# Mean of relu over rows: 126 rows a partition, and two blocks of 128 rows in the first load

## The chip, the cores, the metric

One core of one Trainium2 chip. The metric is the device time of one execution in microseconds (us); the median of several executions is given. Lower is better. The profile's own span begins with the first instruction and ends with the last, and is about 1.3 us shorter than that execution's time (159.8 against 161.13 us for the profiled run of the kernel before).

The kernel spreads its rows over 128 partitions of the on-chip memory (the first number in shapes such as 128x1024). Of the engines, ACT is ScalarE, DVE is VectorE, POOL is GpSimd, and SP is the one that issues the transfers here. A *run* is one contiguous stretch of bytes that one DMA engine moves as one transfer. A *semaphore* is a counter by which a finished load, or a finished instruction, is told to whoever waits for it.

## The reference

```python
# x: (32, 512, 1024) float32, that is 16384 rows of 1024 numbers, 4 KB each
relu_x = np.maximum(x, 0)
return np.mean(relu_x, axis=-1).astype(np.float32)     # (32, 512)
```

67.11 MB are read once, 64 KB are written.

## The kernel before

The first 128 rows are an early block, one row to a partition. Of the other 16256 rows each partition has 127 consecutive ones. They come as seven tiles of 16 rows (a run of 64 KB for each partition, three buffers), then as pieces of 7, 4, 2 and 1 rows, and the last row in three pieces by columns. All loads are issued by the SP engine on one queue. ACT reduces the even rows, DVE the odd ones; the one-row piece (the *split row* below) is shared, 448 columns for ACT and 576 for DVE.

```python
xfirst, xmain = xf[:P, :], xf[P:, :]
outfirst, outmain = out.flatten()[:P], out.flatten()[P:]
J = J - 1                                               # 127
xr = xmain.rearrange("(p j) d -> p j d", p=P, j=J)      # pitch between partitions: 127 rows
...
NB, BUFS = 16, 3                                        # (two lines in the kernel)
full = J // NB                                          # 7
row_pieces = [7, 4, 2, 1]
col_pieces = [512, 256, 256]
...
for t in range(full):
    buf_free(t)                                         # waits for ACT and DVE, from t = 3
    if t == 0:
        load(-1, row0[:, :], xfirst)                    # early block
    load(t, bufs[t % BUFS][:, :, :], xr[:, t * NB:(t + 1) * NB, :])
    if t == BUFS:
        nc.sync.wait_ge(first, 2)
        nc.sync.dma_start(                              # the early block's 128 means
            out=outfirst.rearrange("(q i) -> q i", i=32), in_=turned0[0:P:32, :],
        ).then_inc(stored, 16)
...                                                     # loads of the pieces
nc.scalar.activation(                                   # early block, on ACT
    out=row0[:, :], in_=row0[:, :], func=ACT.Relu, scale=inv, accum_out=mean0[:, 0:1],
).then_inc(first, 1)
nc.vector.wait_ge(first, 1)
nc.vector.transpose(turned0[:, :], mean0[:, :]).then_inc(first, 1)
for t in range(full):
    rows(t, bufs[t % BUFS], 0, NB, t * NB)              # 8 rows on ACT, 8 on DVE
...
dve_row(nc, last[:, 512:768], last[:, D + 1:D + 2]).then_inc(dve, 1)     # "256-wide"
...
nc.vector.scalar_tensor_tensor(                         # the last one: 256 columns and two partial sums
    out=last[:, 768:], in0=last[:, 768:], scalar=0.0, in1=scale[:, :], op0=ALU.max, op1=ALU.mult,
    accum_out=res[:, J - 1:J],
).then_inc(dve, 1)
...
nc.sync.dma_start(out=outr[:, j0:], in_=res[:, j0:]).then_inc(stored, 16)   # last store
```

## Time and profile before

| | before |
|---|---|
| time, three runs | 161.34 us (161.02 to 161.39) |
| span of the profiled run | 159.8 us |
| share of the span: DMA queue, DVE, ACT | 97.9%, 46%, 44% |
| first load byte to last (single transfers) | 1.44 to 157.56 us |
| one 64 KB run, median | 2418 ns |

The shares of a span are averages. "Single transfers" are the records that the trace keeps for each run a DMA engine moved: start, duration, size. They do not name the engine. Their times are given here, and in the prediction, on a scale on which the last record ends with the span. As the trace keeps them they stand 0.40 to 0.45 us earlier on the scale of the timeline (1.01 to 157.13 us for the kernel before). Durations and streams do not depend on this, but the gap between a single transfer and an instruction does.

### The profile page before, as it was taken

Reading aid. Unit: us, or ns where it says so; the run is one execution under the profiler, and the core shown is the slowest. Engines: PE = TensorE matmul, PEld = TensorE weight load, DVE = VectorE, ACT = ScalarE, POOL = GpSimd, SP = SyncE. Lnnn points to the kernel's source line nnn. Section 1 sums busy time; section 2 is a strip of 40 time slices with the busy share of each in tenths; the row PEclk is TensorE's granted clock in tenths of the full one; section 3 lists DMA queues with packets and bytes.
Section 4 is the critical chain, followed back from the end, with each engine's and each line's share of the span. In section 5 each row is a group of like instructions: output and inputs, shape, how many; then the busy total and the mean of one; then the engine's idle time right before and its main releaser. Section 6 shows DMA issues by size and latency. Waiting matters only on the chain. (4 is left out here: it accounts for less than half of the span.)

```text
span 159.8 us, 348 instructions
## 1 busy us (share of the span) xinstructions
DVE 73.3 (46%) x131; ACT 70.4 (44%) x133; POOL 1.3 (1%) x9
## 2 busy tenths in 40 slices
DVE  0000029900399005970079500894009920199975
ACT  1400029800397005950079300892009900199974
POOL 1000000000000000000000000000000000000001
DMA  9979989999799699699699699799899997998993
GB/s 394 459 328 525 410 377 525 394 394 525 345 443 525 263 525 525 263 525 525 263 525 509 279 525 476 312 525 427 361 525 394 394 525 328 427 438 382 414 411 110
DMA packets 2456, 67.18 MB, mean 420 GB/s; under 512 B 536, under 2 KB 792, under 8 KB 1176
## 3 DMA queue, kind: packets, MB, share of 16 engines
q1 hardware_dynamic: 2456, 67.18, 97.9%
HBM read 67.11 MB, written 0.07 MB: 420 GB/s over the span
## 5 line engine op out<-in xcount | busy, mean ns | idle before, releaser
L20 DVE TENSOR_SCALAR_CACHE_REDUCE rows<-rows 128x1024 f32<-128x1024 f32 (+1 forms) x63 | 72.1, 1209 | 78.8 <-DMA rows<-in_x_dram 78.6
L15 ACT ACTIVATE rows<-rows 128x1024 f32<-128x1024 f32 x64 | 66.2, 1035 | 84.0 <-DMA rows<-in_x_dram 83.8
L15 ACT ACTIVATION_READ_ACCUMULATOR rows<-rows 128x1 f32 x64 | 11.9, 186 | 0.0
L20 DVE DVE_READ_ACCUMULATOR rows<-rows 128x1 f32 x63 | 5.2, 83 | 0.0
L168 DVE STREAM_TRANSPOSE turned<-mean 128x32 f32<-128x32 f32 x1 | 0.2, 211 | 5.9 <-ACT row L164 5.9
L164 ACT ACT_TABLE_LOAD x1 | 1.3, 1283 | 3.3 <-DMA row<-in_x_dram 3.3
L157 POOL TENSOR_SCALAR res<-sums 128x112 f32<-128x112 f32 (+1 forms) x2 | 0.5, 249 | 153.8 <-DVE rows L20 153.8
L164 ACT ACTIVATE row<-row 128x1024 f32<-128x1024 f32 x1 | 1.1, 1056 | 0.0
L15 ACT ACTIVATE last<-last 128x512 f32<-128x512 f32 x1 | 0.6, 629 | 0.0
L20 DVE TENSOR_SCALAR_CACHE_REDUCE last<-last 128x256 f32<-128x256 f32 x1 | 0.4, 420 | 0.3 <-DMA last<-in_x_dram 0.3
L197 DVE SCALAR_TENSOR_TENSOR last<-last,scale 128x258 f32<-128x258 f32 x1 | 0.4, 428 | 0.1
L142 POOL MEMSET scale<- 128x258 f32 x1 | 0.3, 313 | 0.0
L187 POOL TENSOR_SCALAR res<-part 128x1 f32<-128x1 f32 x1 | 0.3, 266 | 0.6 <-DVE rows L20 0.6
L164 ACT ACTIVATION_READ_ACCUMULATOR row<-row 128x1 f32 x1 | 0.2, 187 | 0.0
L15 ACT ACTIVATION_READ_ACCUMULATOR last<-last 128x1 f32 x1 | 0.2, 186 | 0.0
L141 POOL MEMSET mean<- 128x32 f32 x1 | 0.1, 125 | 1.5 <-POOLq L55 1.5
L235 POOL MEMSET const-bfloat16-1.0<- 128x1 bf16 x1 | 0.1, 103 | 0.0
L235 POOL MEMSET const-uint8-127<- 128x1 uint8 x1 | 0.1, 103 | 0.0
L235 POOL MEMSET const-float32-0.0<- 128x1 f32 x1 | 0.1, 99 | 0.2 <-issue 0.2
L235 POOL MEMSET const-float32-1.0<- 128x1 f32 x1 | 0.1, 99 | 0.0
L20 DVE DVE_READ_ACCUMULATOR last<-last 128x1 f32 x1 | 0.1, 83 | 0.0
L197 DVE DVE_READ_ACCUMULATOR last<-last,scale 128x1 f32 x1 | 0.1, 82 | 0.0
## 6 DMA issues: line engine op xcount, KB each, us to landing
rows<-in_x_dram SPq DMA_DIRECT2D x1, 3584.0 KB, 37.9
rows<-in_x_dram SPq DMA_DIRECT2D x1, 2048.0 KB, 42.4
rows<-in_x_dram SPq DMA_DIRECT2D x1, 1024.0 KB, 44.5
row<-in_x_dram SPq DMA_DIRECT2D x1, 512.0 KB, 3.2
rows<-in_x_dram SPq DMA_DIRECT2D x1, 512.0 KB, 45.3
last<-in_x_dram SPq DMA_DIRECT2D x1, 256.0 KB, 45.5
last<-in_x_dram SPq DMA_DIRECT2D x2, 128.0 KB, 45.2
rows<-in_x_dram SPq DMA_DIRECT2D x7, 48.7
```

Of the source, the lines that this page charges most:

```text
L15: return nc.scalar.activation(out=src, in_=src, func=ACT.Relu, accum_out=acc)
L20: return nc.vector.tensor_scalar(out=src, in0=src, scalar1=0.0, scalar2=init, op0=ALU.max, op1=ALU.add, accum_out=acc,)
L141: nc.gpsimd.memset(mean0[:, :], 0.0)
L142: nc.gpsimd.memset(scale[:, :], inv).then_inc(pool, 1)
L157: nc.gpsimd.tensor_scalar(out=res[:, lo:hi], in0=sums[:, lo:hi], scalar1=inv, scalar2=0.0, op0=ALU.mult, op1=ALU.add,).then_inc(pool, 1)
L164: nc.scalar.activation(out=row0[:, :], in_=row0[:, :], func=ACT.Relu, scale=inv, accum_out=mean0[:, 0:1],).then_inc(first, 1)
L168: nc.vector.transpose(turned0[:, :], mean0[:, :]).then_inc(first, 1)
L187: nc.gpsimd.tensor_scalar(out=res[:, J - 2:J - 1], in0=part[:, 0:1], scalar1=part[:, 1:2], scalar2=inv, op0=ALU.add, op1=ALU.mult,).then_i ...
L197: nc.vector.scalar_tensor_tensor(out=last[:, 768:], in0=last[:, 768:], scalar=0.0, in1=scale[:, :], op0=ALU.max, op1=ALU.mult, accum_out=r ...
L235: nc = _bacc.Bacc("TRN2", target_bir_lowering=False, num_devices=1)
```

## The change

Intent, as far as the source tells it: one more row of every partition goes into the early load, which makes the rest an even 126 rows and shortens the first piece behind the tiles and the last store.

```diff
-    xfirst, xmain = xf[:P, :], xf[P:, :]
-    outfirst, outmain = out.flatten()[:P], out.flatten()[P:]
-    J = J - 1
+    xfirst, xmain = xf[:2 * P, :].rearrange("(c p) d -> p c d", c=2), xf[2 * P:, :]
+    outfirst, outmain = out.flatten()[:2 * P], out.flatten()[2 * P:]
+    J = J - 2
...
-    row_pieces = [7, 4, 2, 1]
+    row_pieces = [6, 4, 2, 1]
...
-            nc.sync.dma_start(
-                out=outfirst.rearrange("(q i) -> q i", i=32), in_=turned0[0:P:32, :],
-            ).then_inc(stored, 16)
+            for c in range(2):
+                nc.sync.dma_start(
+                    out=outfirst[c * P:(c + 1) * P].rearrange("(q i) -> q i", i=32), in_=turned0[c:P:32, :],
+                ).then_inc(stored, 16)
...
-    nc.scalar.activation(
-        out=row0[:, :], in_=row0[:, :], func=ACT.Relu, scale=inv, accum_out=mean0[:, 0:1],
-    ).then_inc(first, 1)
+    for c in range(2):
+        done = nc.scalar.activation(
+            out=row0[:, c, :], in_=row0[:, c, :], func=ACT.Relu, scale=inv, accum_out=mean0[:, c:c + 1],
+        )
+    done.then_inc(first, 1)
```

(Cut: the shape of `row0`, the argument of the first load, the final count of `stored`.)

More of the change, by code (lines that the diff above doesn't have):

```diff
@@ L88 @@
     scale = sbuf("scale", P, D // 4 + 2)
-    row0, mean0, turned0 = sbuf("row0", P, D), sbuf("mean0", P, 32), sbuf("turned0", P, 32)
+    row0, mean0, turned0 = sbuf("row0", P, 2, D), sbuf("mean0", P, 32), sbuf("turned0", P, 32)
     loaded = [nc.alloc_semaphore(f"loaded{i}") for i in range(full + len(row_pieces) + len(col_pieces) + 1)]
@@ L119 @@
         if t == 0:
-            load(-1, row0[:, :], xfirst)
+            load(-1, row0[:, :, :], xfirst)
         load(t, bufs[t % BUFS][:, :, :], xr[:, t * NB:(t + 1) * NB, :])
@@ L212 @@
     nc.sync.sem_clear(range(used[0], used[-1] + 1))
-    nc.sync.wait_ge(stored, 48).then_inc(stored, -48)
+    nc.sync.wait_ge(stored, 64).then_inc(stored, -64)
     for e, hint in zip(hinted, hints):
```

## The prediction

> **What bounds the kernel now.** I read the busy shares first, then the load queue, then who waits for whom, then the instructions of the last 20 us, and last the single transfers recorded in the trace. The busy shares and the queue, from the page:
>
> ```profile
> DVE 73.3 (46%) x131; ACT 70.4 (44%) x133; POOL 1.3 (1%) x9
> ...
> GB/s 394 459 328 525 410 377 525 394 394 525 345 443 525 263 525 525 263 525 525 263 525 509 279 525 476 312 525 427 361 525 394 394 525 328 427 438 382 414 411 110
> ...
> q1 hardware_dynamic: 2456, 67.18, 97.9%
> ...
> HBM read 67.11 MB, written 0.07 MB: 420 GB/s over the span
> ```
>
> No engine is busy half of the span, while the one load queue keeps the 16 DMA engines busy for 97.9% of it. The swings between 263 and 525 GB/s in the slices come from booking: a row of 64 KB counts when it ends. The waits say the same:
>
> ```profile
> ACT rows L15 <- DMA rows<-in_x_dram: 83.8, 9, 17.2
> DVE rows L20 <- DMA rows<-in_x_dram: 78.6, 8, 16.9
> ...
> SPq L115 <- DVE rows L20: 104.6, 5, 29.5
> ```
>
> ACT and DVE wait on loads for half of the span. The queue's own wait of 104.6 us for a free buffer is harmless: a 16-row load is issued far ahead and lands a median 48.7 us later, against 19.35 us from one tile's first transfer to the next one's (the records put three of them at 22.49, 41.85 and 61.19 us), so more loads always stand behind it.
>
> The records of single transfers settle how full the stream is. The first load byte moves at 1.44 us, the last lands at 157.56 us: 156.11 us. The durations of all load transfers add to 155.96 us per DMA engine, and the semaphore writes add 0.16 us. So there are no holes. The 896 transfers of 64 KB (16 rows for one partition) last 2418 ns at the median and 2426 ns at the mean. What follows the last load is this, from the timeline:
>
> ```profile
> 157.32 0.42 DVE L20 TENSOR_SCALAR_CACHE_REDUCE last<-last 128x256 f32<-128x256 f32 x1 [0.27 <-DMA last<-in_x_dram]
> 157.67 0.08 DVE L20 DVE_READ_ACCUMULATOR last<-last 128x1 f32 x1
> 157.84 0.43 DVE L197 SCALAR_TENSOR_TENSOR last<-last,scale 128x258 f32<-128x258 f32 x1
> 158.19 0.08 DVE L197 DVE_READ_ACCUMULATOR last<-last,scale 128x1 f32 x1
> 158.30 0.34 SPq L208 DMA_DIRECT2D out_dram<-res  x1
> ```
>
> From the last load's end: 0.28 us to the last DVE instruction, 0.46 us to the store's issue, 1.27 us until the store's first packet (159.57) and 0.21 us until its last (159.78). The span of 159.8 us is thus 1.44 before the stream, 156.11 of stream, 2.23 after it. The measured 161.34 us lies 1.5 us above that span.
>
> **What the Trainium skill says.** "DMA: Bandwidth & Descriptors", section "Where 436 GB/s comes from", gives 16 ports of 256 bits at 850 MHz, 435.2 GB/s, as the ceiling. The trace agrees: 65536 B in 2418 ns is 27.10 GB/s an engine, 433.7 GB/s on 16. The full transfers are at that ceiling, so a better layout in memory cannot make them faster.
>
> The same page, "Latency and other measured facts", row on the HBM row pitch, reports that per-partition pitches at large powers of two slow copies (207 GB/s at 512 KiB against 214 for a padded pitch). This bears on the change: the pitch between partitions goes from 127 x 4 KiB = 508 KiB to 126 x 4 KiB = 504 KiB. Neither is a power of two, and no run here yet shows a slow pitch; at 508 KiB the trace shows none.
>
> The same page, "Why a DMA increments its semaphore by 16 and not by 1", says that the slowest dimension decides over how many engines a transfer is spread, 128 partitions giving 16. The new first load keeps 128 partitions outermost, so it should keep 16.
>
> **The change, part by part.** Comparing the two builds' instructions shows the same number of loads, one more store, and otherwise changed shapes.
>
> *Bytes.* All 16384 rows are read once, before and after: 67.11 MB. Nothing is saved.
>
> *Descriptors.* The first load becomes 256 runs of 4 KB instead of 128. From the records, 64 KB take 2418 ns and 8 KB 309 ns at the least: (2418 - 309) / 57344 B = 0.0368 ns a byte, and 309 - 8192 x 0.0368 = 8 ns for the descriptor itself. A 4 KB run at the usual 159 ns agrees (151 + 8). Eight more descriptors per engine cost 8 x 8 = 0.064 us. The 7-row piece becomes 6 rows but keeps its 128 descriptors, so no descriptor is saved elsewhere. Sum in the stream: +0.06 us, all of it on the path, because the stream has no holes.
>
> *Start.* The issue of the first load took 0.39 us. A pattern with twice the runs may take longer to expand; I allow 0 to 0.1 us before the first byte and take 0.03. At the cold start the first 128 runs of 4 KB averaged 185 ns against 159 (0.2 us more per engine), and the first four 64 KB transfers of each engine were together 0.30 us over the floor. I assume that this belongs to the start and not to the kind of transfer, so it moves by nothing.
>
> *ACT and DVE.* ACT gets one more 1024-wide reduction ahead of the tiles (1056 + 187 ns) and one fewer later. The first tile starts at 22.99 us and the early work ends at 6.06 us, so neither touches the end. The transpose, and the store behind it, come about 1.22 us (512 KB at the stream's rate) + 1.1 us later, still far ahead of the fourth load's buffer wait.
>
> *Extra store.* 4 runs of 128 B at 13 ns each, in mid-stream (80.6 us in the records), on four engines: at most 0.02 us each, and about 0.35 us of the load queue's issue time while 64 KB rows are stacked up ahead. Nothing on the path.
>
> *The last pieces.* The last full tile now lands 512 KB later relative to the end, hence 139.12 + 1.22 + 0.06 = 140.40 us. DVE needs 1.14 us a row: 8 rows and then 3 of the six-row piece end at 152.94, where the four-row piece came at 152.51 before. Its two rows end at 155.22, the one row of the two-row piece at 156.36, and its accumulator read at 156.44. The split row then starts about 0.15 us after its 156.29 of before, or 0.1 us after the shifted stream. Ahead of the next DVE instruction stood an idle 0.27 us on a load (157.32), which absorbs that. ACT does three rows of the piece instead of four, and gains room.
>
> *Last store.* 56 B runs instead of 60 B; the records have 8 to 11 ns for each, 8 per engine. Four bytes less in a run is nothing: 0.00 us.
>
> Sum: 0.06 + 0.03 + 0 = +0.09 us on 161.34, so 161.43 us, rounded to 161.4. The size of the change in the source is not the size of its effect: it swaps who carries 128 rows in one continuous stream.
>
> **The rivals.** First, the pitch hurts: 504 KiB shares a larger power of two (8 KiB) than 508 KiB (4 KiB), and 16 engines read rows a multiple of it apart. For it: the skill's row on pitches. Against it: the loads run at the ceiling of the receiving side, so a mild loss behind it stays invisible, and 504 is still padded. If it showed as 1% on the 56 tile transfers of an engine, it would be 1.4 us: 162.8. If 3%, as in the skill's 207 against 214, 4 us: 165.4.
>
> Second, the other way round: the pitch or the longer first load removes what is still lost. For it: the mean of 2426 ns lies 8 ns above the floor, 56 x 8 = 0.45 us per engine, and the cold row adds 0.2 us. Against it: 0.30 us of the 0.45 are the cold start. Even with all of it gone the time is 160.7, so this cannot reach 2% (3.2 us).
>
> Third, the late DVE sets the end: the chain of row starts above is tight at 152.9 and after. If each wait costs 0.1 us more than I assume, four of them make 0.4 us, less the 0.27 us of slack: 161.6.
>
> Fourth, the cold start costs per run of 4 KB, not once: 8 more runs at +26 ns are 0.2 us, giving 161.6.
>
> **Range and chances.** The three runs of before spread over 0.37 us (161.02 to 161.39), more than the effect; the median of before in another session may move by 0.2. Below lies at most the second rival, above the third and fourth and a little of the first. So 161.0 to 161.8 holds 8 in 10. Faster by over 2% would need 158.1, which is less than stream plus issue allow: 1%. Slower by over 2% needs 164.6, only the pitch in its full size: 3%. Within 2%: 96%.
>
> **What would show it.** In the profile after: a span of 159.7 to 160.2; 64 KB transfers still at 2418 ns; the first load landing 1.2 to 1.4 us later than the 3.2 us of before and the first tile's work at about 24.2 instead of 22.99; the last tile's work at about 140.4; DVE still waiting on a load ahead of its 256-wide instruction, with less than 0.27 us. The mechanism is wrong if the 64 KB transfers grow (pitch), if the stream shows holes or starts over 0.2 us later (issue), or if DVE has no wait left at the end (third rival).

## The result, and the profile after

| | before | changed |
|---|---|---|
| first comparison, six runs each | 161.23 us (161.02 to 161.53) | 161.31 us (161.19 to 161.80) |
| span of the profiled run | 159.8 us | 160.0 us |
| first load byte to last | 1.44 to 157.56 us | 1.55 to 157.81 us |
| 64 KB run, median | 2418 ns | 2418 ns |

The ratio is 1.0007, 95% interval 0.999 to 1.0024: the same. A second comparison (e8 below) gave 1.0002, 0.9988 to 1.0016.

From the changed kernel's page, the lines that answer to those of before:

```profile
DVE 73.0 (46%) x131; ACT 70.3 (44%) x133; POOL 1.3 (1%) x9
...
DMA packets 2592, 67.18 MB, mean 420 GB/s; under 512 B 544, under 2 KB 800, under 8 KB 1312
...
q1 hardware_dynamic: 2592, 67.18, 97.9%
```

Same bytes, same 97.9%, and more packets: 2592 against 2456. The difference is 136: 128 more runs of 4 KB, four more runs of the second small store and four more semaphore writes. In the number of packets that is the whole change.

The waits of the changed kernel (engine, line, what it waited for: us in total, times, longest):

```profile
ACT rows L15 <- DMA rows<-in_x_dram: 82.3, 9, 15.9
DVE rows L20 <- DMA rows<-in_x_dram: 76.4, 7, 15.5
...
ACT L166 <- DMA row<-in_x_dram: 5.1, 1, 5.1
```

Both engines still wait on loads for half of the span. The early block lands at 5.1 us, 3.3 before. Then the start, from the timeline (start us, duration us, engine, line, operation):

```profile
0.00 0.45 SPq L109 DMA_DIRECT2D row<-in_x_dram  x1
...
6.36 1.06 ACT L166 ACTIVATE row<-row 128x1024 f32<-128x1024 f32 x1
...
7.42 1.04 ACT L166 ACTIVATE row<-row 128x1024 f32<-128x1024 f32 x1
...
8.66 0.21 DVE L171 STREAM_TRANSPOSE turned<-mean 128x32 f32<-128x32 f32 x1 [8.66 <-ACT row L166]
24.40 1.06 ACT L15 ACTIVATE rows<-rows 128x1024 f32<-128x1024 f32 x1 [15.85 <-DMA rows<-in_x_dram]
```

The second early reduction fills idle time: 15.85 us of waiting remain before the first tile. And the end. Before, both engines took up the four-row piece together, after a wait:

```profile
152.51 1.06 ACT L15 ACTIVATE rows<-rows 128x1024 f32<-128x1024 f32 x1 [0.62 <-DMA rows<-in_x_dram]
152.51 1.22 DVE L20 TENSOR_SCALAR_CACHE_REDUCE rows<-rows 128x1024 f32<-128x1024 f32 x1 [0.77 <-DMA rows<-in_x_dram]
```

In the changed kernel:

```profile
140.51 1.22 DVE L20 TENSOR_SCALAR_CACHE_REDUCE rows<-rows 128x1024 f32<-128x1024 f32 x1 [10.16 <-DMA rows<-in_x_dram]
...
152.71 1.06 ACT L15 ACTIVATE rows<-rows 128x1024 f32<-128x1024 f32 x1 [0.65 <-DMA rows<-in_x_dram]
153.05 0.08 DVE L20 DVE_READ_ACCUMULATOR rows<-rows 128x1 f32 x1
153.05 1.22 DVE L20 TENSOR_SCALAR_CACHE_REDUCE rows<-rows 128x1024 f32<-128x1024 f32 x1
...
156.48 0.75 DVE L20 TENSOR_SCALAR_CACHE_REDUCE rows<-rows 128x576 f32<-128x576 f32 x1
...
157.55 0.42 DVE L20 TENSOR_SCALAR_CACHE_REDUCE last<-last 128x256 f32<-128x256 f32 x1 [0.31 <-DMA last<-in_x_dram]
...
158.07 0.43 DVE L200 SCALAR_TENSOR_TENSOR last<-last,scale 128x258 f32<-128x258 f32 x1
...
158.53 0.34 SPq L211 DMA_DIRECT2D out_dram<-res  x1
```

ACT takes up the four-row piece as soon as it lands (152.71). DVE comes 0.34 us late to it, at 153.05, with no wait, close to the lateness that the prediction worked out (152.94 against 152.51 plus 0.06). It has caught up by the 256-wide instruction, which again waits for a load, 0.31 us.

### The profile page after: what moved, and what is told of

It reads as the page before. It is cut to its first block, busy times and chain, and to the rows that moved or that the text cites. A ratio compares the mean times of both kernels' runs of the same rounds, so it can differ in the third digit from the quotient of the medians.

```text
span 160.0 us, 349 instructions
## 1 busy us (share of the span) xinstructions
DVE 73.0 (46%) x131; ACT 70.3 (44%) x133; POOL 1.3 (1%) x9
## 2 busy tenths in 40 slices
DMA packets 2592, 67.18 MB, mean 420 GB/s; under 512 B 544, under 2 KB 800, under 8 KB 1312
## 3 DMA queue, kind: packets, MB, share of 16 engines
q1 hardware_dynamic: 2592, 67.18, 97.9%
## 5 line engine op out<-in xcount | busy, mean ns | idle before, releaser
L15 ACT ACTIVATE rows<-rows 128x1024 f32<-128x1024 f32 (+1 forms) x63 | 65.2, 1038 | 82.5 <-DMA rows<-in_x_dram 82.3
L166 ACT ACTIVATE row<-row 128x1024 f32<-128x1024 f32 x2 | 2.1, 1050 | 0.0
## 6 DMA issues: line engine op xcount, KB each, us to landing
rows<-in_x_dram SPq DMA_DIRECT2D x1, 3072.0 KB, 36.7
```

What stands on the lines that cost most here:

```text
L15: return nc.scalar.activation(out=src, in_=src, func=ACT.Relu, accum_out=acc)
L166: done = nc.scalar.activation(out=row0[:, c, :], in_=row0[:, c, :], func=ACT.Relu, scale=inv, accum_out=mean0[:, c:c + 1],)
```

## The experiments

All ten gave correct results. "Before" means runs of the kernel before on the same chip in the same session: 161.47 us for e1 to e4, 161.21 for e5 to e8, 161.18 for e9 and e10. Below, the *start excess* is worked out from the single transfers of the first 10 us: what they took beyond the usual duration of their size (159 ns for 4 KB, 2418 ns for 64 KB), added up and divided by 16. *Stream* is the time from the first load byte to the last. The changed kernel's stream was 156.25 us and its start excess 0.70. The trace also keeps the sixteen increments by which each load's semaphore tells of its completion. Read as one from each DMA engine, they show how far apart the engines are; *spread* is the time from the first to the last of the sixteen. In the changed kernel it was 0.39 us for the first tile and 0.37 for the last load.

### e1: what a run costs beside its bytes

```diff
-    bufs = [sbuf(f"rows{b}", P, NB, D) for b in range(BUFS)]
+    bufs = [sbuf(f"rows{b}", P, NB, D + (0 if b == full % BUFS else 8)) for b in range(BUFS)]
```

(and loads and reductions that take only the first D columns). Built on the changed kernel.

> The changed kernel, with the rows of two of the three tile buffers kept 32 bytes apart, so that five of the seven full tiles arrive as 4 KB runs and not as 64 KB runs: 15 x 8 x 5 = 600 more transfers per DMA engine, same bytes. Theory (every transfer costs about 8 ns beside its bytes, and the stream has no holes, so it shows whole): +4.8 us, 166.1 us, 4 KB transfers at 159 ns. Rival (the price of a run is hidden behind its neighbours, or something other than the stream sets the time): 161.3 to 162 us, 4 KB transfers near 151 ns. If it is 170 or more, the producing of the runs is a limit of its own.

Measured: 166.22 us, ratio to before 1.0296 (1.0272 to 1.0320).

```profile
DMA packets 12192, 67.18 MB, mean 407 GB/s; under 512 B 544, under 2 KB 800, under 8 KB 11552
...
q1 hardware_dynamic: 12192, 67.18, 99.3%
```

9600 more packets, 600 for each engine, and a stream of 161.12 us, 4.87 longer: 8.1 ns a run. The prediction's 8 ns holds, and a lengthened stream shows whole in the time. The durations recorded for the 4 KB runs grew to a mean of 163 ns, though, and all load durations add to 163.3 us per engine, more than the stream lasts. Records of short runs on one engine therefore overlap, and their sum is no proof that there are no holes; the length of the stream is the safer measure.

### e2: a pitch of exactly 512 KiB, no early block

```diff
-    xfirst, xmain = xf[:P, :], xf[P:, :]
-    J = J - 1
+    xmain = xf                                  # J = 128, no early load, no early reduction
-    row_pieces = [7, 4, 2, 1]
+    row_pieces = [8, 4, 2, 1]
```

(Shortened: the early block's means, its transpose and its small store go too.)

> No early block at all: 128 rows a partition, so the pitch between partitions is exactly 512 KiB; pieces 8, 4, 2, 1 after the seven tiles. Theory (the loads run at the ceiling of the receiving side and the pitch does not show): 64 KB transfers stay at 2418 ns, 8 transfers per engine fewer than before the change, 161.1 to 161.3 us, or 0.06 us below before and 0.13 below the changed kernel. Rival (the pitch costs rate[...]): 64 KB transfers of 2440 to 2490 ns and 162.7 to 165.5 us. If the rival holds, 504 KiB was merely far enough away from it.

Measured: 161.66 us, ratio to before 1.0015 (0.9997 to 1.0033). 64 KB transfers kept a median of 2418 ns. The rival's 1 to 3% is out. The theory's 161.1 to 161.3 is missed as well, by 0.4 us, or by 0.25 if taken as 0.06 below the 161.47 of its session. Two things stand out in the single transfers: the first byte came at 1.66 us, and two groups of 64 KB transfers in mid-stream (eight starting at 35.9 to 36.7 us, seven at 65.1 to 65.9) took 2500 to 2740 ns. The engines were also far apart, from the first tile (a spread of 0.94 us) to the last load (0.93). e6 follows this up.

### e3: the first tile ahead of the early block

```diff
-        if t == 0:
-            load(-1, row0[:, :, :], xfirst)
         load(t, bufs[t % BUFS][:, :, :], xr[:, t * NB:(t + 1) * NB, :])
+        if t == 0:
+            load(-1, row0[:, :, :], xfirst)
```

> The changed kernel with its first two loads exchanged: the first 16-row tile goes ahead of the 2 x 128 rows. Theory (the slow first microseconds belong to the start, whatever is loaded then; +0.1 us of later first byte belongs to the longer pattern of the first issue): first byte back at 1.44 us, 4 KB transfers of the block at 159 to 161 ns at the mean, the cold excess of 0.5 to 0.7 us per engine now in the first 64 KB transfers, time 161.1 to 161.4. Rival (the cold excess is paid per short run): the block keeps a mean near 200 ns wherever it stands and the first 64 KB transfers are at 2418 to 2440 ns.

Measured: 161.84 us, ratio to before 1.0025 (1.0006 to 1.0045); the expected 161.1 to 161.4 was missed. The mechanism came as the theory said: first byte at 1.47 us, the block's 4 KB runs at a mean of 160 ns, and the start excess of 0.77 us now wholly in the first 64 KB transfers, whose first sixteen averaged 3188 ns, the slowest 3785. The slow start belongs to the start. The time was lost otherwise: the durations of loads and semaphore writes add to 156.35 + 0.16 = 156.51 us per engine, near the 156.27 + 0.16 of the changed kernel, while the stream lasted 156.96 against 156.25. A stream that is 0.45 us longer than its engines' mean work points to some engines that ended later than others. The semaphores show it: the spread was already 1.11 us for the first tile, one engine standing 0.54 us behind the next one, and for the last load it was still 1.04 us, with that engine 0.51 us behind. So the start set one engine back, and nothing behind it let that engine catch up. Why it fell back so far is open.

### e4: sixteen blocks

The change with 16 in place of 2: 112 rows a partition, `row_pieces = [8, 4, 2, 1]`, six tiles, sixteen small stores. The block lands in a tile buffer, as there is no room for another 64 KB, so the third tile's load has to wait for ACT to have reduced the block. That opened no hole: the tiles ahead of the stores land 19.35 us apart, as before.

> The change carried eight times further: 16 blocks of 128 rows in the first load (8 MB in 4 KB runs, landing in a tile buffer), 112 rows a partition, pitch 448 KiB, six full tiles, pieces 8, 4, 2, 1, sixteen small stores. 104 transfers per engine more than the changed kernel. Theory (8 ns a transfer, cold start once): +0.83 us over the changed kernel, 162.1 us, plus 0 to 1 us if the first byte waits for the longer pattern to be expanded. Rival (cold excess of about 40 ns per short run of the first load): +5.4 us, about 167 us. Rival (ACT's sixteen early reductions, about 20 us, or sixteen stores hold something up): holes in the stream, DVE and ACT late at the end.

Measured: 164.31 us, ratio to before 1.0176 (1.0155 to 1.0197), between the theory's 162.1 (163.1 with a late first byte) and the rival's 167. The first byte came at 1.61 us, so it hardly waits for the longer pattern. The stream lasted 159.14 us, 2.89 more than the changed kernel's; 104 runs at 8 ns explain 0.83. The single transfers show another part: four 64 KB transfers, starting at 100.29 to 100.47 us, took 4274 to 4364 ns, 1.9 us too long each. They start right behind the runs of the small stores (100.05 to 100.47 us), which all go to four engines: each such store has four semaphore writes. The semaphores show the same: up to the stores the spread of a load was 0.60 us; from the first load behind them to the last, four of the sixteen engines stood 1.9 to 2.2 us behind the first one and the other twelve at most 0.5. So the sixteen stores do hold something up, but no compute engine: the suspicion is that they stall the four DMA engines that carry them.

### e7: the same means in four stores over sixteen engines

```diff
-            for c in range(16):
-                nc.sync.dma_start(
-                    out=outfirst[c * P:(c + 1) * P].rearrange("(q i) -> q i", i=32), in_=turned0[c:P:32, :],
+            for q in range(4):
+                nc.sync.dma_start(
+                    out=outfirst.rearrange("(c q i) -> q c i", q=4, i=32)[q], in_=turned0[32 * q:32 * q + 16, :],
                 ).then_inc(stored, 16)
```

> e4 with its sixteen small stores of 4 runs each (all on four DMA engines) put together as 4 stores of 16 runs, one run per engine each. Theory (in e4 the sixteen small stores stalled the next 64 KB transfer of those four engines by 1.9 us, and the last of the stream waits for the slowest engine): no 64 KB transfer over 2700 ns in mid-stream, all engines end within 0.6 us of each other, 162.6 to 162.9 us against 164.31. Rival (the 4364 ns transfers are from something else at that time, or the time is lost at the start): 164.1 us or more.

Measured: 162.68 us, ratio to before 1.0094 (1.0080 to 1.0108): 1.6 us faster than e4 (1.3 us if each is compared by its ratio to the before of its session), with the same 64 runs stored. The slowest 64 KB transfer in mid-stream took 2551 ns, and the spread stayed where it was, 0.68 us for the first tile and 0.63 for the last load. Bandwidth of e4 and then of e7 in 40 slices of the span, each from its own page:

```profile
GB/s 225 389 419 408 411 463 515 515 257 515 515 273 499 515 370 402 515 386 386 515 434 338 515 483 292 450 515 306 466 515 322 450 515 354 418 410 398 414 365 35
```

```profile
GB/s 225 401 410 415 410 477 520 455 325 520 455 325 520 455 325 520 455 325 520 455 325 520 455 325 522 455 325 520 455 325 520 455 325 520 357 422 382 425 404 104
```

The last slice of e4 holds only 35 GB/s, against 104 in e7: most engines were done while four were still behind. (The swings before it say nothing of the stores. A row of 64 KB counts whole in the slice in which it starts, and five rows of 2.42 us fill three slices of e7's 4.03 us, which makes its pattern repeat, but not three of e4's 4.07.) So the stall came from piling sixteen small stores on the same four engines. Two things stay open. The edit also cut the number of store instructions from sixteen to four, though no more than four engines fell behind. And the stall does not grow in step with the number of stores: with two (the changed kernel) and four (e5) no 64 KB transfer beside them took over 2428 ns, and the sixteen runs and semaphore writes of an engine add up to only 0.35 us by their records.

What is left of e7 over the changed kernel (162.68 against 161.26 in the same session, 1.42 us) is 0.83 us of runs and a start excess that is 0.38 us higher (0.88 against 0.50 in e8), with a further 0.33 us of slow 4 KB runs between 10 and 25 us. The terms add to 1.54 us, 0.12 more than there is, as records of short runs that overlap can. A long phase of short runs thus has some excess of its own, far less than the fourth rival's 26 ns a run: about 0.7 us over 112 more runs is 6 ns, or less.

### e5: four blocks

The change with 4 in place of 2, `row_pieces = [4, 4, 2, 1]`, block in a tile buffer (with the wait of e4).

> The change carried to 4 blocks of 128 rows (124 rows a partition, pieces 4, 4, 2, 1 behind the seven tiles; the block lands in a tile buffer for want of room). Theory (third rival of the prediction made real: every block moves the last full tile 1.22 us nearer to the end, and DVE needs 1.14 us a row): the last tile's DVE work starts at 143.1 us and runs without a pause to the split row, which starts near 158.6 in place of 156.5; DVE has no wait on a load left at the end and the kernel ends 1.1 us later than the changed one, 162.3 to 162.6 us, while the last load lands within 0.4 us of the 157.8 of the changed kernel. Rival (the stream alone sets the end): 161.3 to 161.7 us, with a wait of DVE on a load ahead of its 256-wide instruction.

Measured: 162.66 us, ratio to before 1.0091 (1.0076 to 1.0106).

```profile
143.31 1.22 DVE L20 TENSOR_SCALAR_CACHE_REDUCE rows<-rows 128x1024 f32<-128x1024 f32 x1 [10.15 <-DMA rows<-in_x_dram]
...
158.13 0.75 DVE L20 TENSOR_SCALAR_CACHE_REDUCE rows<-rows 128x576 f32<-128x576 f32 x1
158.80 0.08 DVE L20 DVE_READ_ACCUMULATOR rows<-rows 128x1 f32 x1
158.80 0.41 DVE L20 TENSOR_SCALAR_CACHE_REDUCE last<-last 128x256 f32<-128x256 f32 x1
159.14 0.08 DVE L20 DVE_READ_ACCUMULATOR last<-last 128x1 f32 x1
159.32 0.43 DVE L203 SCALAR_TENSOR_TENSOR last<-last,scale 128x258 f32<-128x258 f32 x1
```

No line here after 143.31 has a wait in brackets: DVE runs through from the last tile to the end, 13 full rows at 1.14 us. Its last instruction starts at 159.32 and not at 158.07, 1.25 us later, and the span is 1.24 us longer than the changed kernel's (161.27 against 160.03). The last load landed at 158.17, 0.37 later, inside the expected 0.4. The split row started 0.5 us earlier than expected (158.13; I had written its end, 158.6, for its start), and the time lies 0.06 above the expected 162.6. The third rival is real at four blocks. At two the load was still waited for; whether three would reach it, no run tells.

### e6: the pitch alone

The kernel before, with the early block taken as row 0 of every partition, so that the pitch is 512 KiB with the same sequence of loads:

```diff
-    xfirst, xmain = xf[:P, :], xf[P:, :]
+    xall = xf.rearrange("(p j) d -> p j d", p=P)
+    xfirst, xr = xall[:, 0, :], xall[:, 1:, :]
```

(its means go straight into the column 0 of the ordinary result; no transpose, no small store).

> The kernel before with the early block taken as row 0 of every partition: 128 rows a partition and a pitch of exactly 512 KiB, but the same sequence and sizes of loads as before; the early means go out with the ordinary stores, so transpose and small store fall away. Theory (pitch without effect; the +0.19 us or so of e2 over before came from starting with 64 KB transfers): same as before within 0.2 us, 64 KB transfers at 2418 ns. Rival (the pitch costs a little, seen in e2 as groups of 64 KB transfers of 2550 to 2740 ns in mid-stream on half of the engines): such groups again, +0.2 to +0.5 us over before.

Measured: 161.68 us (161.22 to 161.74), ratio to before 1.0016 (1.0003 to 1.0030). The groups of slow transfers of e2 did not come back in the one execution traced, so the pitch alone does not bring them. 64 KB transfers: median 2418 ns, and from the second tile on means of 2418 to 2424. A higher start excess was there, 0.97 us, in the run that was profiled, and a spread of 0.86 us for the first tile and 0.79 for the last load. The five runs fall into two groups (161.22 and 161.34; 161.68, 161.72 and 161.74), as the eleven of before fell in the session of e1 to e4 (five at 161.05 to 161.20, six at 161.47 to 161.85). Whether the 0.16% is the pitch at work in the start or the luck of five runs stays open. For the change it settles what matters: even at exactly 512 KiB the full transfers do not slow down.

### e8 and e9: both kernels again

> The changed kernel once more, for more rounds and a second trace. Theory: ratio to before 1.000 to 1.002; first byte between 1.4 and 1.7 us, first byte and slow first transfers together differing from the first trace by some 0.1 to 0.3 us, so that the single difference of 0.25 us between the two first traces cannot be split into a start part and a descriptor part by them alone. Rival (the +0.11 us of first byte and the +0.2 us of cold excess are real parts of the change): both repeat within 0.05 us and the ratio is 1.002 or more.

> The kernel before once more, as a run of its own, for a second trace and a null comparison. Theory (the start of the stream differs from execution to execution): time 161.1 to 161.6, ratio to itself within 0.15% of 1; first byte 1.4 to 1.7 us; the excess of the transfers of the first 8 us over their usual durations between 0.3 and 1.0 us per engine, and not the 0.49 of the first trace. Rival (before has a steadily cheaper start than the changed kernel, 0.49 against 0.70 and 0.50 us in its two traces): 0.45 to 0.55 us again.

Neither has an edit. e8: 161.26 us, ratio 1.0002 (0.9988 to 1.0016). e9: 161.18 us, ratio of before to itself 1.0003 (0.9990 to 1.0017). The traces:

| | before, 1st | before, e9 | changed, 1st | changed, e8 |
|---|---|---|---|---|
| span, us | 159.8 | 160.3 | 160.0 | 160.0 |
| first load byte, us | 1.44 | 1.46 | 1.55 | 1.56 |
| start excess, us | 0.49 | 0.52 | 0.70 | 0.50 |
| load durations per engine, us | 155.96 | 155.99 | 156.27 | 156.08 |
| stream, us | 156.11 | 156.39 | 156.25 | 156.23 |
| spread, first tile, us | 0.55 | 0.89 | 0.39 | 0.28 |
| spread, last load, us | 0.44 | 1.09 | 0.37 | 0.27 |

Two traces of the unchanged kernel differ by 0.27 us in the stream and 0.5 us in the span, more than before and after do. e9's traced execution is one of its longer ones (161.66 us), and its engines were further apart from the first tile on. Its last DVE instruction waits for the last load, which it does not do in the other three traces:

```profile
158.38 0.43 DVE L197 SCALAR_TENSOR_TENSOR last<-last,scale 128x258 f32<-128x258 f32 x1 [0.36 <-DMA last<-in_x_dram]
```

This bears on the two groups of e6. The traced executions of e2, e3, e6 and e9, at 161.66 to 161.97 us, have a spread of 0.8 to 1.1 us for the last load; those of before, changed, e8 and e10, at 161.13 to 161.53, have 0.3 to 0.6. So even with the kernel unchanged (before and e9) the slower execution goes with engines that stand further apart from the start on. For executions without a trace this can't be checked.

Of the start excess, that of before is steady (0.49, 0.52), as e9's rival had it; that of the changed kernel is not (0.70, 0.50), against e8's rival. e10, whose start is that of the changed kernel, has 0.36. The first byte comes about 0.1 us later in both traces of the changed kernel (0.09 and 0.08 on the timeline's own scale), and so it does in e1 and e10, with the same first load. The later byte goes with a longer issue (0.45 us against 0.39), but not in proportion: e4's and e7's first loads have eight times as many runs and began at 1.61 and 1.51 us.

e3's stream of 156.96 us lies 0.57 above the longest of these four, which is why its loss is not put down to chance alone; but e9 shows that an engine can fall back without its edit too.

### e10: a shorter last instruction

```diff
-    col_pieces = [512, 256, 256]
+    col_pieces = [512, 384, 128]
```

(with DVE's two last instructions cut to match). Built on the changed kernel, to see whether a better one is within reach.

> The changed kernel with the last row's columns loaded as 512, 384, 128 in place of 512, 256, 256, to see what can be had behind the stream. Theory: the stream ends as before; the last DVE instruction is 128 columns shorter, 0.43 to about 0.30 us, and starts on the last load unless the 384-wide one, about 0.13 us longer, holds it up: 0.05 to 0.15 us faster than the changed kernel, 161.1 to 161.3 us, not to be told from it by the times. Rival (the 384-wide instruction then sets the end): 0 to 0.1 us slower.

Measured: 161.59 us, ratio to before 1.0023 (1.0010 to 1.0037).

```profile
157.71 0.55 DVE L20 TENSOR_SCALAR_CACHE_REDUCE last<-last 128x384 f32<-128x384 f32 x1 [0.43 <-DMA last<-in_x_dram]
158.19 0.08 DVE L20 DVE_READ_ACCUMULATOR last<-last 128x1 f32 x1
158.36 0.29 DVE L200 SCALAR_TENSOR_TENSOR last<-last,scale 128x130 f32<-128x130 f32 x1
```

The rival won in direction: the span is 0.16 us longer than the changed kernel's, and the median time 0.3 to 0.4 us above the changed kernel's 161.26 and 161.31 and the 161.18 of before, more than the rival's 0.1. The 384-wide instruction starts 0.16 us later, as its load has more to bring, and takes 0.13 us longer; the last instruction starts 0.29 us later and gives back 0.14. The last load did not set the end in the changed kernel either. There the last instruction started 0.52 us after the 256-wide one had (157.55 to 158.07), just as in the kernel before (157.32 to 157.84), and the last load had been complete at 157.83. Here it is 0.65 us after the 384-wide one, with the last load complete at 158.03. The path runs through the next-to-last load and DVE, and the edit gave both of them more to do. No experiment pointed to a version that beats both kernels.

## Why the prediction was right

The measured 161.31 us lies 0.1 us from the predicted 161.4, and the difference of +0.08 beside the predicted +0.09. With an interval of about 0.27 us on either side the measurement cannot confirm such a sum, and an agreement to 0.01 us is luck; the experiments confirm its terms, or not.

- **The stream bounds the kernel.** Shown by e1: 4.87 us more of stream made 4.86 us more of span (164.89 against 160.03). The argument by which the prediction got there, that the durations add up to the stream exactly, was weaker than it looked: in before's second trace the stream is 0.24 us longer than the sum, and in e1 the loads' sum is 2.2 us longer than the stream. Two readings on the way were off. The GB/s of a slice count a 64 KB row where it starts, not when it ends: the first slice's 394 GB/s over 3.99 us are 1.57 MB, the early block and sixteen such rows, which all end past 5 us. And the parts of the span, 1.44 and 2.23 us beside the stream, hang on the scale chosen for the transfers; on the timeline's own they are 1.01 and 2.66, with the same sum.
- **8 ns a run, +0.06 us.** e1 measured 8.1 ns.
- **+0.03 us for a later first byte.** The two pairs of traces say 0.08 to 0.11. Undersized by 0.05 to 0.08 us, at the upper end of the 0 to 0.1 that the prediction allowed. With it the sum would be about +0.15 us, which the measurement does not exclude.
- **Cold start unmoved.** e3 shows that it belongs to the start and not to the kind of transfer. Its amount is 0.49 and 0.52 us before, 0.70 and 0.50 after: no shift shown. The new first load is told complete by sixteen increments from the DMA engines, as the old one was, so it kept all sixteen. The excess did move from one load to the other, which the prediction missed: the early block's 4 KB runs averaged 201 ns instead of 185, and the first sixteen 64 KB transfers 2438 instead of 2590. So the block landed 1.8 us later (5.07 against 3.30) and not the 1.2 to 1.4 predicted, which nothing waits for.
- **ACT and DVE at the start.** The first tile's work begins at 24.40 us (predicted about 24.2), and the early work ends at 8.87, far ahead of it.
- **The last pieces.** The last tile's DVE work begins at 140.51 us (predicted 140.40), DVE comes to the four-row piece at 153.05 (predicted 152.94), the split row starts 0.19 us later than before (predicted 0.15). The prediction also had the wait ahead of the 256-wide instruction shrink below 0.27 us; it grew to 0.31, because that load too was complete later (157.53 against 157.30), which the prediction had left out there. It also counted the tail from the last load; in both kernels the next-to-last one set it, by way of DVE (e10). As all loads shift together, this does not change the sum.
- **Small stores on no path.** True for two of them: all 64 KB transfers beside them took 2426 ns at most. As a rule it is false: sixteen on the same four engines cost 1.3 to 1.6 us (e4 against e7).
- **The rivals.** Pitch: out (e2, e6), apart from an open 0.16%. Gain from a better start: none seen. Late DVE: real at four blocks, not at two (e5). Cold start per run: about 6 ns in long phases (e7), not 26.

Left open: why some executions start with their engines further apart, which in the traces goes with the slower of the two groups, some 0.5 us apart, and with e3's loss; and from what number on small stores stall an engine.

## What to carry to other kernels

When one load queue is busy from the first byte to the last at the DMA engines' ceiling, rearranging which rows go in which load is worth the number of runs times their overhead (here 8 ns), the first byte, and what stands behind the last; work these three out before trying. Look twice at what such a change does at the end: each row moved ahead brings the last full tile nearer to the end, and DVE's lateness grows with it until it takes over. And small stores in the middle of a stream are free only while they do not pile up on the same few DMA engines, since the last byte waits for the slowest engine.

## What the Trainium skill lacked or had wrong

- "DMA: Bandwidth & Descriptors", "Why small descriptors are slow (HBM only)": it gives a fixed overhead of about 3 cycles a packet, without naming the clock; at the fabric's 850 MHz that would be 3.5 ns (an estimate from that page). e1 shows 8.1 ns for each 4 KB run in an otherwise full stream, in which other fixed costs may be contained.
- The same page, "Latency and other measured facts", row pitch: 207 GB/s at 512 KiB against 214 at a padded pitch, for copies between HBM tensors. For loads of one core with 64 KB runs, 512 KiB shows none of it in the full transfers: 2418 ns at the median in e2 and e6, as at 504 and 508 KiB; times +0.15 and +0.16%, cause open.
- The same page does not say what small stores that pile up on few engines cost the long loads behind them: sixteen stores on four engines made the next 64 KB transfer of each 4274 to 4364 ns long in place of 2418 (e4); spread over sixteen engines, 2551 at most (e7).
- No page says how unsteady the start of a stream is: first byte to last of one and the same kernel was 156.11 and 156.39 us, and its engines stood 0.55 and 0.89 us apart at the first tile (first trace and e9).
- No page says outright that the recorded durations of short transfers overlap: in e1 they add to 163.3 us per engine within a stream of 161.1.
